# RWKV chain of a hybrid encoder layer: outputs in one group, whole-array products, inverses from 16-row blocks

## The chip, the cores and the metric

The kernel runs on one core of a Trainium2 chip, as one program. The metric is the device time of one execution in microseconds (us), lower is better; three executions of the kernel before are on record, with their median. Engines of the core: TensorE (PE, with its weight loads shown apart as PEld), VectorE (DVE), ScalarE (ACT), GpSimd (POOL) and SyncE (SP, which here only issues DMAs).

## The reference

One layer of an encoder over 256 tokens of width 2048, in float32: a projection, three mixers A, B and C, a gated merge, an output projection and a SwiGLU block. The change touches mixer C alone, RWKV-7 time mixing with 16 heads of 64 channels, once forward and once backward over the tokens:

```python
def step(s, inp):
    r_t, w_t, k_t, v_t, a_t, b_t = inp
    sa = jnp.einsum('dbhij,dbhj->dbhi', s, a_t)
    s = s * w_t[..., None, :] + sa[..., :, None] * b_t[..., None, :] + v_t[..., :, None] * k_t[..., None, :]
    return s, jnp.einsum('dbhij,dbhj->dbhi', s, r_t)
_, y = lax.scan(step, s0, (r, w, k, v, a, b))
...
y = norm_last(y, GN_EPS).reshape(bsz, seq, C_W) * ln_g + ln_b
out = (y + bonus) * g
```

## The kernel before, in words

The kernel has stages in a row: mixer A, mixer B, mixer C (`rwkv`), the last part of the merge (`merge_last`), the output projection, the feed-forward block. Weights come from DRAM in pieces of 128x512 (`wsplit`, L217): SP issues the load, ACT rounds the piece to its high part `wh` (L225), DVE or POOL subtracts to get the low part `wl` (L229). A dense step (`dense`, L233) is three products of 256 columns on the whole array, L242 to L244. Those of mixer C's own projections and of the merge of branch B fill the gaps of the scan: they are called dense below.

The scan is worked out in chunks of 64 tokens, four chunks, for eight pairs of heads (j from 0 to 7), both directions d together. For a pair, in turn:

- `wkv_prep` (L526) makes decays, keys and the arrays `bk` and `ar`; its products L547 use 64 rows of the array, one direction after the other.
- `wkv_scores` (L618) makes the 64x64 score blocks `sc` of all chunks: eight products for a direction (L635), four of one head in 64 rows of the array and then four of the other head; then the blocks go to DRAM (L652).
- `wkv_inverse` (L667) inverts 32x32 diagonal blocks on DVE, a block on a partition: 31 steps k, two instructions each (L688, L689), from a copy `N` loaded at L679. The results go to DRAM (L694), come back as `XX` (L699) and are transposed (L702).
- `wkv_chain` (L707) joins them to 64x64 inverses `XF` by 32x32 products (L731, L742), and then walks the four chunks: L770 (scores times v) and, from the second chunk on, L777 (`ar` times the state) make `Pm`; L785 multiplies by the inverse and gives `UV`; L796 gives what is added to the state, which DVE writes to `sb` (L811, L813); L816 and, from the second chunk on, L819 give the chunk's outputs, which go to `y2` (L824, L826). The products use halves or quarters of the array. L816 and L819 alternate, head by head and direction by direction.
- `wkv_norm` (L833): group norm by two products with a constant (L842, L848), bonus and gate.

These five are generators. `threads` (L481) takes turns between them, and after each yield emits its share of four dense steps a round (`ROUND`), so the order of emission is a round-robin. The framework moves instructions further: the order on an engine is the one that the program ends with. Waits between pieces are the calls of `after`. PSUM tiles come from rings of two, by tag: `big`, `ch`, `inv`, `dn`. `N`, `Y`, `XX`, `UV` have one buffer.

Of the kernel before, what the change touches and what calls it, by code (L numbers as in the profile page):

```python
# [48 lines left out]
for _n, _w in VEC:  # L49
# [6 lines left out]
    ("smask", 256), ("dmask", 64), ("rowm", 2), ("scanm", 257),  # L56
# [11 lines left out]
def shape_constants():  # L68
# [17 lines left out]
    put("rowm", np.stack([blk == 0, blk == 1], 1))  # L86
    put("scanm", np.broadcast_to((np.arange(T + 1) % CH != 0)[None], (P, T + 1)))
# [21 lines left out]
def dft_tables():  # L109
    """odd frequencies (2 k + 1) pi / (2 T), k < T / 2; even and odd samples apart"""  # L110
# [21 lines left out]
def layout(inp):  # L132
# [54 lines left out]
    o["rows"] = np.eye(32).reshape(8, 4, 32).transpose(1, 0, 2)[:, None] * np.ones((1, 32, 1, 1))  # L187
    o["rows"] = o["rows"].reshape(P, 8, 32)
# [5 lines left out]
class Build:  # L194
# [21 lines left out]
    # weights [P, nk, n] from DRAM -> (wh, wl)  # L216
# [16 lines left out]
    def dense(self, ap, xh, xl, ps):  # L233
        """ps[n, t] = sum_k w[k, n] x[k, t]; ap DRAM [P, nk, 128], xh/xl [P, nk, 256]; yields after each k"""
# [48 lines left out]
    def fill(self, n):  # L283
        """emits n steps of the waiting dense products"""
# [26 lines left out]
    def rsqrt_steps(self, x, w, v):  # L311
        """w * -RS_B = x ** -0.5 (x > 0): bit estimate and two Newton steps"""
# [74 lines left out]
    def rwkv(self, rp, ych, ycl, y):  # L387
# [9 lines left out]
        # kd = k (1 + (a - 1) k_a) = k (ka1 (2 a - 1) + ka0)  # L397
# [14 lines left out]
        R["sb"] = []  # L412
        for i in range(2):
            x = rp.tile([P, 2, P], F32, name=f"sb{i}")
            nc.gpsimd.memset(x, 0.0)
            R["sb"].append(x)
# [17 lines left out]
        def more():  # L434
            """the next merge, the queue being short"""
# [45 lines left out]
    def threads(self, live, more):  # L481
        """takes turns between the generators, with dense steps between: more where fewer have something to do"""
# [19 lines left out]
    def weave(self, gens, steps, lead=0):  # L502
        """takes turns between the generators (a pair (n, gen) starts n turns late), with some of `steps` dense ones between"""
# [895 lines left out]
```

## Time and profile before

| | |
|---|---|
| three executions | 2071.43, 2072.45 (median), 2075.77 us |
| span of the profiled execution, first to last instruction | 2081.1 us |
| PE busy in that span | 1985.2 us (95%) |
| DVE busy | 1468.4 us (71%) |
| ACT, POOL busy | 1020.5 us (49%), 552.9 us (27%) |
| mean granted clock of TensorE | 0.965 |

No time of the profiled execution beside its span is on record; the span is 8.65 us above the median of the three. Mixer C's scan lies at about 505 to 1103 us of the span, the merge's last part and everything behind it after 1103 us. A busy PE is not a PE at its peak: a product counts as busy from its start to its end, and its successors overlap it. What a group of products costs is read from starts, not from busy time.

### The profile page before, as it was taken

What the parts mean: (1) busy time and instruction counts of PE and PEld (TensorE: products, weight loads), DVE (VectorE), ACT (ScalarE), POOL (GpSimd) and SP (SyncE); (2) the same over time, 40 slices, a digit from 0 to 9 for tenths busy, and PEclk for the clock granted to TensorE, in tenths of its full rate; (3) what the DMA queues carried; (4) which work ended last, traced back from release to release, by engine and by line L of the source; (5) the groups of instructions that cost most, each with busy time, mean ns of one, the idle gap of its engine ahead of it and who ended that gap; (6) DMA issues with size and microseconds to landing.
All of it is one profiled execution on the core that took longest, in us unless ns stands there. A gap on an engine that the chain in (4) does not pass through costs nothing. (4 is left out here: it accounts for less than half of the span.)

```text
span 2081.1 us, 37899 instructions
## 1 busy us (share of the span) xinstructions
PE 1985.2 (95%) x13636; PEld 1762.9 (85%) x13636; DVE 1468.4 (71%) x2852; ACT 1020.5 (49%) x1982; POOL 552.9 (27%) x557
## 2 busy tenths in 40 slices
PE   7999999999888888999999999999999999999997
PEld 5899999999777777877778888888888888888886
DVE  7968788765887786776766667766666666655555
ACT  5655555545333343333335555555555555544543
POOL 5322322325643443453441121111111111100001
PEclk9999999999888999898899999999999999999998
DMA  7454444345332233332324556555555555566664
GB/s 235 153 173 151 133 161 150 127 157 175 121 103 84 86 106 94 106 103 74 107 91 161 186 197 219 186 191 189 192 189 191 189 190 190 190 186 187 186 187 137
DMA packets 200325, 324.35 MB, mean 156 GB/s; under 512 B 45766, under 2 KB 49352, under 8 KB 200136
## 3 DMA queue, kind: packets, MB, share of 16 engines
q1 hardware_dynamic: 193904, 310.33, 45.9%
q0 software_dynamic: 1888, 5.93, 0.9%
q10 hardware_dynamic: 4344, 5.67, 0.8%
q8 instruction: 107, 1.75, 0.4%
q14 instruction: 82, 0.67, 0.1%
HBM read 317.65 MB, written 4.19 MB: 155 GB/s over the span
## 5 line engine op out<-in xcount | busy, mean ns | idle before, releaser
L225 ACT CAST wh<-w 128x512 fp32r<-128x512 f32 x1148 | 705.0, 619 | 693.8 <-PE ps_dn L262 259.6
L229 DVE TENSOR_TENSOR wl<-w,wh 128x512 fp32r<-128x512 f32 x945 | 709.0, 755 | 370.0 <-ACT wh L225 366.2
L242 PE MATMUL ps_dn<-hw,wh 128*128 128x256 f32 x1328 | 407.4, 307 | 2.3 <-ACT th L1269 1.2
L229 POOL TENSOR_TENSOR wl<-w,wh 128x512 fp32r<-128x512 f32 x203 | 273.2, 1349 | 454.7 <-ACT wh L225 432.2
L244 PE MATMUL ps_dn<-hw,wl 128*128 128x256 f32 x1328 | 388.8, 293 | 1.3 <-DVE wl L229 1.3
L243 PE MATMUL ps_dn<-hw,wh 128*128 128x256 f32 x1328 | 389.7, 293 | 0.0
L242 PEld LDWEIGHTS ps_dn<-hw,wh 128*128 128x128 f32 x1328 | 264.5, 199 | 18.6 <-issue 8.5
L243 PEld LDWEIGHTS ps_dn<-hw,wh 128*128 128x128 f32 x1328 | 265.1, 200 | 4.3 <-issue 1.7
L244 PEld LDWEIGHTS ps_dn<-hw,wl 128*128 128x128 f32 x1328 | 264.7, 199 | 3.7 <-DVE wl L229 1.5
L262 PE MATMUL ps_dn<-gw,wh 128*128 128x512 f32 x704 | 246.3, 391 | 0.0
L262 PE MATMUL ps_big<-gw,wh 128*128 128x512 f32 x704 | 246.0, 391 | 0.0
L262 PE MATMUL ps_dn<-hid,wh 128*128 128x512 f32 x660 | 233.2, 396 | 0.0
L263 PE MATMUL ps_dn<-hid,wl 128*128 128x256 f32 x704 | 198.4, 282 | 0.0
L263 PE MATMUL ps_dn<-gw,wl 128*128 128x256 f32 x704 | 197.3, 280 | 0.0
L263 PE MATMUL ps_big<-gw,wl 128*128 128x256 f32 x704 | 197.1, 280 | 0.0
L262 PEld LDWEIGHTS ps_dn<-gw,wh 128*128 128x128 f32 x704 | 131.7, 187 | 28.9
L262 PEld LDWEIGHTS ps_big<-gw,wh 128*128 128x128 f32 x704 | 131.6, 187 | 28.9
L262 PEld LDWEIGHTS ps_dn<-hid,wh 128*128 128x128 f32 x660 | 124.0, 188 | 30.2
L263 PEld LDWEIGHTS ps_dn<-gw,wl 128*128 128x128 f32 x704 | 133.1, 189 | 0.1
L263 PEld LDWEIGHTS ps_big<-gw,wl 128*128 128x128 f32 x704 | 133.1, 189 | 0.0
L263 PEld LDWEIGHTS ps_dn<-hid,wl 128*128 128x128 f32 x704 | 132.2, 188 | 0.0
L1328 POOL TENSOR_TENSOR acc<-acc,sq 128x256 f32<-128x256 f32 x28 | 20.8, 744 | 291.3 <-ACT sq L1326 283.3
(383 smaller groups left out, 3499.0 us busy)
## 6 DMA issues: line engine op xcount, KB each, us to landing
w<-in_wgu_dram SPq DMA_DIRECT2D x352, 256.0 KB, 3.0
w<-in_wgt_dram SPq DMA_DIRECT2D x192, 256.0 KB, 3.0
w<-in_wdn_dram SPq DMA_DIRECT2D x176, 256.0 KB, 2.9
w<-in_wc_dram SPq DMA_DIRECT2D x108, 256.0 KB, 3.0
w<-in_wb_dram SPq DMA_DIRECT2D x96, 256.0 KB, 3.0
w<-in_wbr_dram SPq DMA_DIRECT2D x96, 256.0 KB, 2.7
w<-in_wo_dram SPq DMA_DIRECT2D x64, 256.0 KB, 3.1
w<-in_wav_dram SPq DMA_DIRECT2D x32, 256.0 KB, 3.9
```

Source lines behind the costliest of these rows:

```text
L225: nc.scalar.copy(wh[:, :m], w[:, :m])
L229: e.tensor_tensor(wl[:, :m], w[:, :m], wh[:, :m].bitcast(F32), ALU.subtract)
L242: mm(ps, wh[:, i, :], xh[:, k, :], start=(k == 0), stop=False)
L243: mm(ps, wh[:, i, :], xl[:, k, :], start=False, stop=False)
L244: mm(ps, wl[:, i, :], xh[:, k, :], start=False, stop=(k == nk - 1))
L262: mm(ps, wh[:, i, :], xk.rearrange("p a t -> p (a t)"), start=(k == 0), stop=False)
L263: mm(ps[:, :T], wl[:, i, :], xk[:, 0, :], start=False, stop=(k == nk - 1))
L1328: self.nc.gpsimd.tensor_tensor(acc, acc, s, ALU.add)
```

## The change

Mixer C alone is changed; line numbers of the changed code differ from those of before.

```diff
-        R["sb"] = []
-        for i in range(2):
-            x = rp.tile([P, 2, P], F32, name=f"sb{i}")
+        R["sb"] = [rp.tile([P, 2, P], F32, name=f"sb{i}") for i in range(3)]
+        R["ar"] = [rp.tile([P, 2, NC_, 3, CH], F32, name=f"ar{i}") for i in range(2)]
+        for x in R["sb"] + R["ar"]:
             nc.gpsimd.memset(x, 0.0)
+        R["d2"] = [self.dp.tile([32, 2, 8, 2, 32], F32, name=f"d2{i}") for i in range(2)]
+        none = rp.tile([P, 256], F32, name="none", tag="kd")
+        nc.gpsimd.memset(none, 0.0)
+        for x in R["d2"]:
+            nc.gpsimd.dma_start(x.rearrange("a b c r e -> (a b c r e)").rearrange("(p f) -> p f", p=P), none)
...
+        pd = [self.pst("big") for _ in range(2)]
+        for i in range(2):
+            for d in range(2):
+                rows = slice(64 * d, 64 * d + 64)
+                nc.tensor.matmul(pd[d][:, i * T:(i + 1) * T], wa[rows, i, :],
+                                 R["lo"][rows, 1 + i, :], start=True, stop=True, tile_position=(64 * d, 0))
...
+            ph = [self.pst("big") for _ in range(2)]
+            for c in range(NC_):
+                for h in range(2):
+                    rows = slice(64 * h, 64 * h + 64)
+                    nc.tensor.matmul(ph[h][:, c * P:(c + 1) * P], bk[rows, d, c // 2, (c % 2) * P:(c % 2) * P + P],
+                                     ar[rows, d, c, 1 - c % 2::1 + c % 2, :], start=True, stop=True, tile_position=(64 * h, 0))
...
-        src = d1.rearrange("d u (q s) e -> (d u q) (s e)", s=32)
+        src = d1.rearrange("d u (q s) e -> (d u q) s e", s=32)
         for i in range(4):
-            D.dma_start(N[32 * i:32 * i + 32].rearrange("p s e -> p (s e)"), src)
+            b = 16 * (i % 2)
+            D.dma_start(N[32 * i:32 * i + 32], src[:, b:b + 16, b:b + 16])
...
-        for k in range(31):
-            n, w = 31 - k, k // 4 + 1
+        for k in range(15):
+            n, w = 15 - k, k // 2 + 1
...
+        V.transpose(Z[:, 1].rearrange("p a b -> p (a b)"), Z[:, 0].rearrange("p a b -> p (a b)"))
+        blocks = [(d, u, q) for d in range(2) for u in range(4) for q in range(4)]
+        ps = self.pst("inv")
+        for d, u, q in blocks:
+            r, o = slice(32 * q, 32 * q + 32), slice(32 * u, 32 * u + 32)
+            nc.tensor.matmul(ps[r, P * d + 32 * u:P * d + 32 * u + 32], Mo[r, d, o], Z[r, 1, d, o], start=True, stop=True,
+                             tile_position=(32 * q, 32 * q))
+        T0 = tl([2, P], "T0")
+        S.copy(T0, ps[:, :2 * P].rearrange("p (d n) -> p d n", d=2))
+        yield 1
...
+            if i:
+                for d, c in at_step(i):
+                    nc.tensor.matmul(pv[:, :P], ar[:, d, c, 0:2, :], R["sb"][i - 1][:, d, :], start=False, stop=(d == 1))
...
+            if i < 3:
+                pv = of_v(i + 1)
...
+                for d, c in at_step(i):
+                    nc.tensor.matmul(ct[:, P * d:P * d + P], bkT[:, d, c, :], UV[:, d, c // 2, c % 2, :], start=True, stop=True)
...
-            for d, c, h in us:
-                o = ct[64 * h:64 * h + 64, 64 * d:64 * d + 64]
-                nc.tensor.matmul(o, UV[:, d, c // 2, c % 2, 64 * h:64 * h + 64], sc[:, d, h, c, CH:], start=True,
-                                 stop=(i == 0), tile_position=(0, 64 * h))
-                if i:
-                    nc.tensor.matmul(o, St[64 * h:64 * h + 64, d, 64 * h:64 * h + 64], ar[64 * h:64 * h + 64, d, c, 1, :],
-                                     start=False, stop=True, tile_position=(64 * h, 64 * h))
...
+        ps = self.pst("big")
+        for i in range(1, NC_):
+            for d, c in at_step(i):
+                nc.tensor.matmul(ps[:, c * CH:(c + 1) * CH], R["sb"][i - 1][:, d, :], ar[:, d, c, 2, :],
+                                 start=(i == 1 and d == 0), stop=False)
+        for i in range(NC_):
+            for d, c in at_step(i):
+                for h in range(2):
+                    nc.tensor.matmul(ps[64 * h:64 * h + 64, c * CH:(c + 1) * CH], UV[:, d, c // 2, c % 2, 64 * h:64 * h + 64],
+                                     sc[:, d, h, c, CH:], start=False, stop=(i == 3 and d == 1), tile_position=(0, 64 * h))
+        y2 = tl([T], "y2")
+        S.copy(y2, ps[:, :T])
```

In words. The outputs of all four chunks are computed behind the chain, in one group: six products with the state on the whole array (L861 in the changed code), then sixteen on halves of the array (L866). The product with the state inside the chain (L819 there) and the one that makes the state's addition (L841 there) use all 128 rows and columns; `ar` has a zero block beside each `a` for that, and the states of three chunks are kept. The products of the two heads (L650 there) and of the two directions (L554 there) alternate between the two halves of the array's rows, into two `big` tiles. `of_v` (L809 there) makes the next chunk's first product right behind the inverse's (L828 there). The inverses are started from 16x16 blocks: 15 steps on DVE instead of 31, loads of `N` in pieces of 16 elements, writes of `d2` in pieces of 16, and two more groups of thirty-two 32x32 products (L730 and L738 there) with a copy on ACT between them, `Mo` being made by two POOL instructions a pair. The gate's product moves from `wkv_prep` to `wkv_norm`, where DVE multiplies by it out of PSUM; POOL did that before. POOL clears `sb`, the two `ar` tiles and `d2` once, ahead of the first pair.

On PE, in the sixth pair, the third chunk of the kernel before reads so (dense rows stand ahead of it and behind):

```order
L244 MATMUL ps_dn<-yb,wl 128x256
L770 MATMUL ps_ch<-UV,sc 64x64 x4
L777 MATMUL ps_ch<-sb_6468,ar 64x128
L816 MATMUL ps_ch<-sc,UV 64x64
L819 MATMUL ps_ch<-ar,sb_6470 64x64
L816 MATMUL ps_ch<-sc,UV 64x64
L819 MATMUL ps_ch<-ar,sb_6470 64x64
L816 MATMUL ps_ch<-sc,UV 64x64
L819 MATMUL ps_ch<-ar,sb_6470 64x64
L816 MATMUL ps_ch<-sc,UV 64x64
L819 MATMUL ps_ch<-ar,sb_6470 64x64
L777 MATMUL ps_ch<-sb_6468,ar 64x128
```

The outputs stood between the products of the two directions with the new state, L777. In the changed program the same place of PE holds only the inverse's product and the next chunk's first one, and then four dense steps:

```order
L245 MATMUL ps_dn<-hw,wl 128x256
L828 MATMUL ps_inv<-T_11902,xf 64x64 x4
L809 MATMUL ps_ch<-UV,sc 64x64 x4
L243 MATMUL ps_dn<-hw,wh 128x256
L244 MATMUL ps_dn<-hw,wh 128x256
L245 MATMUL ps_dn<-hw,wl 128x256
```

L841 and L819 follow in the same way, two rows of 128x128 each, with four dense steps behind each. What moved is the output group, which now stands behind the pair's last chunk on PE:

```order
L245 MATMUL ps_dn<-hw,wl 128x256
L861 MATMUL ps_big<-ar_6472,sb_6468 128x64 x2
L861 MATMUL ps_big<-ar_6472,sb_6469 128x64 x2
L861 MATMUL ps_big<-ar_6472,sb_6470 128x64 x2
L866 MATMUL ps_big<-sc,UV 64x64 x16
L243 MATMUL ps_dn<-hw,wh 128x256
```

At the end of the scan 27 dense steps stand behind the last gate product (L891 in the changed code). On SP, the loads of the first pair's blocks read so before:

```order
L652 DMA d_7114<-Md 128x4x32
L652 DMA d_7114<-Mu 128x4x32
L224 DMA w<-in_wc_dram 128x512 x2
L679 DMA N<-d_7114 32x1024 x4
L224 DMA w<-in_wc_dram 128x512 x5
```

And in the changed program, at the same place of SP:

```order
L670 DMA d_7125<-Md 128x4x32
L670 DMA d_7125<-Mu 128x4x32
L225 DMA w<-in_wc_dram 128x512
L701 DMA N<-d_7125 32x16x16 x4
L225 DMA w<-in_wc_dram 128x512 x5
```

The four loads of `N` stay four, behind the same stores; each moves 32x16 pieces of 16 elements where it moved 32 pieces of 1024.

## Rows read from the trace of the kernel before

**Rows 1.** The page: TensorE's granted clock in 40 slices, tenths.
```profile
PEclk9999999999888999898899999999999999999998
```
**Rows 2.** Windows: length, busy us (instructions) of PE, PEld, DVE, ACT, POOL; clock, DMA.
```profile
505.00:1103.00 598.00, 537.20 (x4453) 459.86 (x4452) 446.06 (x1145) 217.15 (x476) 264.89 (x255) 0.90 0.32 98
```
**Rows 3.** Lines of PE, 505 to 1103 us: busy, mean ns, idle before, releasers.
```profile
L816 PE MATMUL ps_ch<-sc,UV 128*64 128x64 f32 x256 | 37.7, 259 | 9.1 <-DVE sb L811 6.1 <-DVE sb L813 2.0 <-ACT UV L791 0.7
...
L777 PE MATMUL ps_ch<-sb,ar 128*64 128x128 f32 x96 | 19.8, 332 | 9.0 <-DVE sb L811 7.4 <-DVE sb L813 1.7
```
**Rows 4.** Timeline of PE: start us, us, engine, line; a state's addition among dense products.
```profile
1021.70 0.28 PE L242 MATMUL ps_dn<-yb,wh 128*128 128x256 f32 x1
1021.82 0.28 PE L243 MATMUL ps_dn<-yb,wh 128*128 128x256 f32 x1
1022.03 0.46 PE L796 MATMUL ps_ch<-UV,bkT 128*64 128x64 f32 x8
1022.42 0.39 PE L244 MATMUL ps_dn<-yb,wl 128*128 128x256 f32 x1
1022.64 0.28 PE L242 MATMUL ps_dn<-yb,wh 128*128 128x256 f32 x1
```
**Rows 5.** Timeline of PE: the outputs of one chunk.
```profile
1050.94 0.33 PE L816 MATMUL ps_ch<-sc,UV 128*64 128x64 f32 x2
1051.19 0.33 PE L819 MATMUL ps_ch<-ar,sb 64*64 64x64 f32 x2
...
1053.21 0.28 PE L244 MATMUL ps_dn<-yb,wl 128*128 128x256 f32 x1
```
**Rows 6.** Timeline of PE: both kinds of 64x64 products together.
```profile
1086.12 0.27 PE L770 MATMUL ps_ch<-UV,sc 64*64 64x64 f32 x2
1086.14 0.27 PE L785 MATMUL ps_ch<-Pm,xf 64*64 64x64 f32 x2
...
1086.74 0.28 PE L243 MATMUL ps_dn<-hw,wh 128*128 128x256 f32 x1
```
**Rows 7.** Timeline of PE: four transposes of 128 columns on the whole array.
```profile
579.19 0.60 PE L661 MATMUL ps_big<-consts,bk 128*128 128x128 f32 x4
...
579.74 0.28 PE L243 MATMUL ps_dn<-hw,wh 128*128 128x256 f32 x1
```
**Rows 8.** Timeline of PE: the scores of one direction.
```profile
856.63 1.88 PE L635 MATMUL ps_big<-ar,bk 64*128 64x128 f32 x16 [2.08 <-DVE sc L637]
...
858.67 0.28 PE L243 MATMUL ps_dn<-hw,wh 128*128 128x256 f32 x1
```
**Rows 9.** Timeline of PE: the products of one direction's decays.
```profile
886.40 1.13 PE L547 MATMUL ps_big<-lo,wa 64*128 64x256 f32 x4
...
887.68 0.28 PE L243 MATMUL ps_dn<-hw,wh 128*128 128x256 f32 x1
```
**Rows 10.** Timeline of PE: sixteen 32x32 products, two passes each.
```profile
1072.56 0.45 PE L742 MATMUL ps_inv<-XX,T 32*32 32x32 f32 x32
...
1073.17 0.28 PE L244 MATMUL ps_dn<-hw,wl 128*128 128x256 f32 x1
```
**Rows 11.** Lines of DVE, 505 to 1103 us: busy, mean ns, idle before.
```profile
L689 DVE TENSOR_TENSOR Y<-Y,Yt 128x60 f32<-128x60 f32 (+24 forms) x248 | 95.1, 383 | 4.0
```
**Rows 12.** Timeline of DVE: the state of one chunk.
```profile
1088.02 1.19 DVE L811 SCALAR_TENSOR_TENSOR sb<-ps_ch,E,ws 64x64 f32<-64x64 f32 x4 [0.96 <-PE ps_ch L796]
```
**Rows 13.** Tile N: durations ns min/median/max, first and last start us; landing of its loads.
```profile
L688 DVE TENSOR_TENSOR Yt<-N,Y x248: 142/214/4892, 563.7 to 1059.1; 128x60 f32<-128x60 f32 x12, 128x54 f32<-128x54 f32 x8, 128x66 f32<-128x66 f32 x8, 128x28 f32<-128x28 f32 x8
L679 SPq DMA_DIRECT2D N<-d x32: 325/420/597, 554.9 to 1013.8; - x32
...
DMA to landing us min/median/max: 2.1/3.4/6.2
```
**Rows 14.** DMA issues, 505 to 1103 us: KB each, median us to landing.
```profile
XX<-d SPq DMA_DIRECT2D x8, 128.0 KB, 3.3
...
d<-Md SPq DMA_DIRECT2D x8, 64.0 KB, 1.8
```

More of the change, by code (lines that the diff above doesn't have):

```diff
@@ L186, in layout @@
     o["cst"], o["csw"] = shape_constants()
-    o["rows"] = np.eye(32).reshape(8, 4, 32).transpose(1, 0, 2)[:, None] * np.ones((1, 32, 1, 1))
-    o["rows"] = o["rows"].reshape(P, 8, 32)
+    o["rows"] = np.eye(16).reshape(8, 2, 16).transpose(1, 0, 2)[:, None] * np.ones((1, 64, 1, 1))
+    o["rows"] = o["rows"].reshape(P, 8, 16)
     o["feat"] = filter_features()
@@ L542, in wkv_prep @@
         sm = self.cst("scanm")
-        for d in range(2):
-            rows = slice(64 * d, 64 * d + 64)
-            ps = self.pst("big")
-            for i in range(2):
-                nc.tensor.matmul(ps[:, i * T:(i + 1) * T], wa[rows, i, :],
-                                 R["lo"][rows, 1 + i, :], start=True, stop=True, tile_position=(64 * d, 0))
+        pd = [self.pst("big") for _ in range(2)]
[4 more added lines that the diff above has]
+                                 R["lo"][rows, 1 + i, :], start=True, stop=True, tile_position=(64 * d, 0))
+        for d in range(2):
+            ps = pd[d]
             tw = tl([T], "tw")
@@ L760, in wkv_chain @@
         self.passed.add(("v", j))
[L763 to L782 removed]
+        at_step = lambda i: [(d, i if d == 0 else 3 - i) for d in range(2)]
@@ new lines, in wkv_chain @@
+        pv = of_v(0)
+        for i in range(NC_):
+            if i:
+                for d, c in at_step(i):
+                    nc.tensor.matmul(pv[:, :P], ar[:, d, c, 0:2, :], R["sb"][i - 1][:, d, :], start=False, stop=(d == 1))
+            Pm = tl([P], "T1")
+            V.tensor_copy(Pm, pv[:, :P])
+            yield 1
+            ct = self.pst("inv")
+            for h in range(2):
+                for d, c in at_step(i):
+                    hb = 1 - c % 2
+                    rows = slice(64 * hb, 64 * hb + 64)
+                    nc.tensor.matmul(ct[rows, 64 * h:64 * h + 64], XF[rows, d, h, c // 2, :, :],
+                                     Pm[rows, 64 * h:64 * h + 64], start=True, stop=True, tile_position=(64 * hb, 64 * hb))
+            if i < 3:
+                pv = of_v(i + 1)
+            for d, c in at_step(i):
@@ L783, in wkv_chain @@
                 hb = 1 - c % 2
                 rows = slice(64 * hb, 64 * hb + 64)
-                nc.tensor.matmul(ct[rows, P + 64 * h:P + 64 * h + 64], XF[rows, d, h, c // 2, :, :],
-                                 Pm[rows, 64 * h:64 * h + 64], start=True, stop=True, tile_position=(64 * hb, 64 * hb))
-            for d in range(2):
-                c = i if d == 0 else 3 - i
-                hb = 1 - c % 2
-                rows = slice(64 * hb, 64 * hb + 64)
-                (S.copy if d else V.tensor_copy)(UV[rows, d, c // 2, c % 2, :], ct[rows, P:2 * P])
+                (S.copy if d else V.tensor_copy)(UV[rows, d, c // 2, c % 2, :], ct[rows, :P])
@@ L792, in wkv_chain @@
             yield 1
             if i < 3:
[L794 to L802 removed]
+                ct = self.pst("inv")
@@ L848, in wkv_norm @@
         nc.tensor.matmul(ps[:, :T], self.cst("bones"), sq2, start=True, stop=True)
+        pg = self.pst("big")
+        nc.tensor.matmul(pg[:, :T], g2, R["lo"][:, 0, :], start=True, stop=True)
         yield 1
```

138 lines of the change are left out of this document (65 added, 73 removed).

## The prediction

> **What bounds the kernel now.** First the granted clock over the span: it dips below full in the second quarter and is full behind it [rows 1]. That stretch is mixer C's scan, so the windows are asked for it alone: of 598 us PE is busy 537.2, so it stands idle for 60.8 us; DVE is busy 446.06, ACT 217.15, POOL 264.89, at a mean clock of 0.90 [rows 2]. PE is the busiest, but it is not full of dense work. The dense products there are 720 steps of three (24 columns of weights of mixer C and 16 of the merge, less what is emitted ahead of the first pair), and one product follows another after 0.12 us at full clock [rows 4]; that makes 259 us. The other half of the stretch goes to the scan's small products, to waits, and to the lower clock. The clock has two levels, 1.2 and 2.4 GHz; a mean of 0.90 says that a fifth of the stretch ran at the lower. So the question is what a small group costs the dense stream, and for that the timeline of PE is read by starts, at full clock, among dense products.
>
> I count as the price of a group the time from its start to the start of the second dense product behind it, less 0.12 for that product's own place, plus 0.09 for the entry where the array is divided. The entry is seen in [rows 4]: the group starts 0.21 us behind a dense product instead of 0.12. Its price is 0.61 - 0.12 + 0.09 = 0.58 for eight passes (a float32 product is two). The outputs of one chunk, sixteen passes, cost 2.27 - 0.12 + 0.09 = 2.24 [rows 5]: the two kinds of products alternate, and a new kind starts 0.25 us behind the last. Sixteen passes of two kinds on different quarters, which start 0.02 us apart, cost 0.62 - 0.12 + 0.09 = 0.59, as much as eight [rows 6]. Four passes of 128 columns on the whole array cost 0.55 - 0.12 = 0.43, 0.11 each, taken without an entry [rows 7].
>
> **The change part by part.** *The chain.* Before, a pair has four groups L785, three L796, four L770, two times three L777 and the first chunk's L816: 18 groups, at 0.58 10.4 us; with three output groups of 2.24 it is 17.1. Where two groups stand together one entry is paid, so I take 16.3. After: the first L809 and the last L828 0.58 each; three groups of L828 with L809, between 0.59 (both kinds at once, [rows 6]) and 1.16 (one behind the other), I take 0.8; L841 and L819 three times each, four passes on the whole array, 0.43 [rows 7]. Outputs: twelve passes of 64 columns on the whole array, each between half of the 0.11 and 0.11, together 0.6 to 1.3, I take 1.0; 32 passes on halves, between 1.2 (sixteen couples at 0.06 and one entry and exit of 0.25) and four groups of 0.58, 2.3; they stand together as eight passes do in [rows 4], so I take 1.3. Sum 0.58 + 0.58 + 2.4 + 2.6 + 2.3 = 8.5. Saved 7.8 a pair, 62 us in all (bounds 6.2 and 9 a pair).
>
> The Trainium skill, "TensorE: Matmul & The Clock Gate", section "LDWEIGHTS (loading the stationary operand)", speaks against whole-array products here: a load's time goes by the columns of weights, so a block with another head's half in it pays for all 128. By its rate a pass of the state's output would cost 0.107 us whatever the 64 columns that stream, 1.3 us for twelve, and the sum would be 2 us lower. [Rows 7] agree with that rate at 128 columns; no row here shows 64 columns behind 128 of weights.
>
> *Scores.* One direction costs 2.04 - 0.12 + 0.09 = 2.01 [rows 8], 0.11 a pass with 0.25 for entry and exit. Alternating between halves of the rows the sixteen passes are eight couples: 8 x 0.11 + 0.25 = 1.13 if the halves run at once as the quarters do in [rows 6], 2.01 if not. I take 1.13: 0.88 twice a pair, 14 us in all; bound 0. *Decays.* A direction costs 1.28 - 0.12 + 0.09 = 1.25 [rows 9]; both in one group of four couples cost about one of them: 10 us saved, and 2 if only an entry goes.
>
> *Inverses.* On PE two groups of 64 passes are new. Thirty-two passes cost 0.61 - 0.12 + 0.09 = 0.58 [rows 10]; 64 between that and 1.16, I take 0.95: 15 us more in all. On DVE 32 instructions a pair go, 256 of some 0.38 us (L689 [rows 11]; L688, its twin, has half of the instructions): 97 of its 446 us. The new transpose, addition and gate product are some 0.4 us each, and four small additions to the outputs go: nothing in sum.
>
> PE's work at full clock falls by 62 + 14 + 10 - 15 = 71 us. Divided by the stretch's 0.90 it is 79 (bounds: 33 / 0.9 = 37 with every upper price, 87 / 0.9 = 97 with every lower).
>
> *Waits.* PE's idle 60.8 us: the outputs waited 9.1 us, mostly for the state on DVE [rows 3]; they now stand behind the chain, where the states are long there. Of the other 51.7 most are waits for DVE, whose work shrinks by a fifth: 11 us less. Against it stands an added wait. L819 of the changed code needs the states of both directions; before, the outputs' 2.24 us stood between the two halves of L777, which still waited 9.0 us [rows 3]. DVE's four instructions take 1.19 us [rows 12], and four dense steps, 1.44 us, now stand between L841 and L819. That covers them when DVE is free; where another thread's work stands ahead of them, all that is queued on PE, dense products too, waits up to another 1.19 us. In 24 chunks that is 0 to 29 us; I take 10, as the threads other than the chain have work for about a third of the rounds. Waits: -9 - 11 + 10 = -10, bounds -30 and +20.
>
> *At nothing.* The gate's product only moves on PE. POOL's clearing at the start: a mean POOL instruction takes 264.89 / 255 = 1.04 us, so even at three times that for each of the two large ones, with the stores behind them, it is under 10 us once; POOL is idle for half of the stretch and weights are split three pieces ahead; without that cover PE would wait those 10 us. The last pair's norm is covered by the dense steps behind it, 27 x 0.36 = 9.7 us.
>
> **Sum.** 79 + 10 = 89 us. Against the profiled span: 2081.1 - 89 = 1992. That span is 8.65 us above the median; the same 89 off the median give 2072.45 - 89 = 1983, rounded up to 1984. The likeliest case's own range is 1955 to 2015: prices from 60 to 97, waits from -20 to +5.
>
> **Rivals.** *The waits take it back* (1 in 6). With less small work between them, the chain's links (copy of `Pm`, `UV`, state) wait for DVE and ACT more often. For: every link is a round, and a round has four dense steps whatever else is in it; [rows 8] show a wait of 2.08 us for a `big` tile, and the scores now take both `big` tiles at once. Against: DVE loses 97 us. At 50 us of new waits the time is 2034.
>
> *The clock opens* (1 in 8). At the lower level the stretch loses about a tenth of its time. For: the clock is full in the quarter behind it [rows 1], where PE does nothing but whole-array work, and much of the divided-array work goes. Against: waits of 2 us stay. If half of the lower-clock time goes, another 25 us and some of the waits' bound go with it: 1950.
>
> *Slower: the loads of N* (1 in 12). A load of `N` moves the same blocks in 2048 pieces of 64 bytes, where it was 128 long ones. DVE is in order, so if `N` lands late, the chain's copies behind the first L709 wait, and PE for them. Today a load lands after 3.4 us (at most 6.2) and DVE starts on it 563.7 - 554.9 = 8.8 us behind its issue [rows 13]. Stores and loads in small pieces: 512 pieces land in 1.8 us, 1024 in 3.3 [rows 14], so 1.5 us for 512 more, and 2048 would take 6.3: inside the 8.8. To eat 89 us over eight pairs each load must be 11 us late, that is land after 20. At 22 us the time is 2072.45 - 89 + 8 x (22 - 8.8) = 2089. The Trainium skill, "DMA: Bandwidth & Descriptors", section "Specifications", is the reason to list it: it wants pieces of 512 bytes or more and says that smaller ones are read, modified and written. By that alone the loads are several times dearer; the trace's store of 128-byte pieces that lands in 1.8 us bears the rule out only weakly.
>
> *Nothing* (1 in 33): a cause outside PE's order holds the stretch; ACT at 217 of 598 us and the loads do not look like one [rows 2]. Time 2072.
>
> **How the numbers follow.** Forecast 0.6, waits 0.17, clock 0.12, nothing 0.03, slower 0.08. A measurement of this kernel tells 0.2%, 4 us, from no change. The waits' case is faster but for a small part: faster 0.88, same 0.04, slower 0.08. The range reaches from 1945 (half of the clock's case) to 2035 (half of the waits' case); outside are about 0.05 below and 0.15 above.
>
> **What would show it.** Right: the scan's stretch falls from 598 us to about 509; the output group costs 2 to 3 us once a pair; L650 starts in couples; L819's wait stays under 20 us in all; DVE's busy time there falls by nearly 100. Wrong: the stretch's idle time on PE above 80 us, L650 with starts 0.11 apart one by one, the first L709 idle for a DMA, or the clock's mean far from 0.90 either way.

## The result and the profile after

Four executions of the changed kernel took 2008.69 to 2020.24 us, median 2014.29; the kernel before, beside it, 2073.57. The ratio is 0.9715, 95% interval 0.9683 to 0.9747: faster by 59 us, where 89 were forecast, and inside the range. A second set of six executions (after_again, below) gave 0.9692 (0.9667 to 0.9716), 64 us. The spans of the profiled executions, 2018.2 us and 2081.1 before, differ by 62.9. A profile is of one execution, and those of the changed kernel lie up to 14 us apart (both of its profiles are of the slowest), so a few microseconds between two profiles tell little.

The granted clock by slices, from the page of the changed kernel, answers to [rows 1]:

```profile
PEclk8999999999889899898999999999999999999999
```

The scan now ends at 1039.2 us, where the first product of the merge's last part starts; it ended at 1103. Its window, with the columns of [rows 2]:

```profile
505.00:1039.20 534.20, 472.05 (x5275) 430.62 (x5274) 374.65 (x885) 213.32 (x453) 269.66 (x281) 0.91 0.35 101
```

The reader is to see three things. The whole gain lies here: 598.0 - 534.2 = 63.8 us, and what follows takes 979.0 us against 978.1. PE's busy time fell from 537.20 to 472.05, by 65.2. Its idle time did not fall: 60.8 before, 534.2 - 472.05 = 62.2 after. DVE lost 71.4 us of busy time, and the mean clock is 0.91 against 0.90.

Busy time is not work when the clock changes. By the clock rows of the traces PE was busy at the lower of its two levels, 1.2 GHz, for 121.1 us before and 82.6 after. With that time counted half, PE's work at full clock is 537.2 - 60.5 = 476.7 us before and 472.1 - 41.3 = 430.8 after. So the 63.8 us are 46 of PE's work, 19 of less time at the lower level, and -1.4 of idle time.

PE's lines in that window, with the idle time ahead of each and what ended it, answer to [rows 3]:

```profile
L650 PE MATMUL ps_big<-ar,bk 64*128 64x128 f32 x256 | 36.0, 327 | 7.4 <-DVE bon L625 5.7 <-DVE bk L610 1.2 <-ACT ta L561 0.3
L819 PE MATMUL ps_ch<-sb,ar 128*128 128x128 f32 x96 | 21.3, 330 | 17.8 <-DVE sb L853 14.9 <-DVE sb L855 2.6
L841 PE MATMUL ps_inv<-UV,bkT 128*128 128x128 f32 x96 | 17.7, 306 | 11.6 <-DVE UV L835 11.6
...
L730 PE MATMUL ps_inv<-Z,Mo 32*32 32x32 f32 x512 | 6.6, 204 | 8.0 <-DVE Z L725 8.0
```

The state's addition to `Pm` (L819) waits 17.8 us, as much as the outputs and L777 waited together, 9.1 + 9.0. The waits for `UV` (L841) and for the returned inverses `Z` (L730) make 19.6 of the other 44.4 us; the rest is spread over many lines, none above 7.4 us.

The output group of a pair, from PE's timeline, answers to [rows 5]:

```profile
1022.49 1.45 PE L861 MATMUL ps_big<-ar,sb 128*128 128x64 f32 x12
1023.87 1.15 PE L866 MATMUL ps_big<-sc,UV 128*64 128x64 f32 x32
1024.95 0.39 PE L243 MATMUL ps_dn<-hw,wh 128*128 128x256 f32 x1
1025.17 0.28 PE L244 MATMUL ps_dn<-hw,wh 128*128 128x256 f32 x1
```

By the prediction's measure (to the second dense product, less its 0.12) it costs 1025.17 - 1022.49 - 0.12 = 2.56 us, once a pair. Twelve whole-array passes take 1.38, or 0.115 each with the change of kind: 64 streamed columns did not make these passes cheaper than the 0.11 of 128 columns in [rows 7]. By the Trainium skill's page "TensorE: Matmul & The Clock Gate", section "LDWEIGHTS (loading the stationary operand)", a weight load's time goes by the columns of weights, for 128 of them an estimate of 0.107 us. The trace agrees with that.

The scores come in two ways. From the same timeline, half of a group of one direction whose heads do not alternate, and then a whole group whose heads do, answer to [rows 8]:

```profile
943.93 1.16 PE L650 MATMUL ps_big<-ar,bk 64*128 64x128 f32 x8
945.02 0.38 PE L243 MATMUL ps_dn<-yb,wh 128*128 128x256 f32 x1
...
954.66 1.17 PE L650 MATMUL ps_big<-ar,bk 64*128 64x128 f32 x16
955.76 0.39 PE L243 MATMUL ps_dn<-hw,wh 128*128 128x256 f32 x1
955.98 0.28 PE L244 MATMUL ps_dn<-hw,wh 128*128 128x256 f32 x1
```

Sixteen passes take 1.10 us as couples, eight take 1.09 one by one. Seven of the 16 groups alternate from end to end, two in part, seven not at all: the program alternates, but the order that the framework ends with lets the first head's products pass and holds the second's. I read that as places where only one `big` tile is free; it is not shown by itself. The order on PE in such a place (tile numbers kept; in the trace one begins at 645.32 us):

```
4219 L650 MATMUL ps_big_8399<-ar0_6471,bk_8246 128x128
4220 L828 MATMUL ps_inv_8370<-T1_8352,xf_8192 64x64 x4
4221 L650 MATMUL ps_big_8399<-ar0_6471,bk_8246 128x128 x3
...
4231 L650 MATMUL ps_big_8400<-ar0_6471,bk_8246 128x128 x4
```

The inverse's two lines on DVE, answering to [rows 11], and then tile `N`, answering to [rows 13]:

```profile
L710 DVE TENSOR_TENSOR Y<-Y,Yt 128x30 f32<-128x30 f32 (+10 forms) x120 | 47.3, 394 | 2.7
L709 DVE TENSOR_TENSOR Yt<-N,Y 128x30 f32<-128x30 f32 (+10 forms) x120 | 34.4, 286 | 10.8 <-DMA N<-d 8.6
```

```profile
L709 DVE TENSOR_TENSOR Yt<-N,Y x120: 145/184/1260, 561.7 to 980.6; 128x30 f32<-128x30 f32 x24, 128x14 f32<-128x14 f32 x16, 128x24 f32<-128x24 f32 x16, 128x15 f32<-128x15 f32 x8
...
DMA to landing us min/median/max: 2.1/2.8/3.6
```

The two lines take 81.7 us for the 187.8 of before (95.1, and 92.7 of L688); an instruction is hardly shorter in the mean, though most take 0.18. The loads in 64-byte pieces land after 2.8 us, the long ones after 3.4; each also moves a quarter of the bytes, 32 KB where it was 128.

### The profile page after: what moved, and what is told of

Read it like the earlier page. It is cut to its first block, busy times and chain, and to the rows that moved or that the text cites. A ratio compares the mean times of both kernels' runs of the same rounds, so it can differ in the third digit from the quotient of the medians.

```text
span 2018.2 us, 39307 instructions
## 1 busy us (share of the span) xinstructions
PE 1920.9 (95%) x14468; PEld 1734.5 (86%) x14468; DVE 1397.8 (69%) x2588; ACT 1017.0 (50%) x1958; POOL 562.2 (28%) x587
## 4 chain that ended last, share of the span: by engine, by line
PE 82%; DVE 11%; DMA 3%; issue 2%; ACT 1%; SPq 0%; POOL 0%; DVEq 0%; ACTq 0%; POOLq 0%
PE ps_dn L263 23%; PE ps_dn L264 12%; PE ps_dn L243 9%; PE ps_big L263 8%; PE ps_dn L244 8%; PE ps_dn L245 8%; PE ps_big L264 4%; DVE Y L710 2%; PE ps_big L650 1%; DVE wl L230 1%; DVE Yt L709 1%; DMA Z<-d 1%; PE ps_ch L819 1%; PE ps_big L981 0%; DMA N<-d 0%
## 5 line engine op out<-in xcount | busy, mean ns | idle before, releaser
L230 DVE TENSOR_TENSOR wl<-w,wh 128x512 fp32r<-128x512 f32 x945 | 711.4, 758 | 381.6 <-ACT wh L226 377.8
L243 PE MATMUL ps_dn<-hw,wh 128*128 128x256 f32 x1328 | 402.5, 303 | 1.6 <-ACT th L1312 1.2
L245 PE MATMUL ps_dn<-hw,wl 128*128 128x256 f32 x1328 | 382.9, 288 | 1.9 <-DVE wl L230 1.9
L244 PE MATMUL ps_dn<-hw,wh 128*128 128x256 f32 x1328 | 381.9, 288 | 0.0
L230 POOL TENSOR_TENSOR wl<-w,wh 128x512 fp32r<-128x512 f32 x203 | 273.3, 1350 | 383.9 <-ACT wh L226 345.0
L243 PEld LDWEIGHTS ps_dn<-hw,wh 128*128 128x128 f32 x1328 | 259.5, 195 | 12.4 <-issue 4.0
L245 PEld LDWEIGHTS ps_dn<-hw,wl 128*128 128x128 f32 x1328 | 259.5, 195 | 3.2 <-DVE wl L230 2.1
L244 PEld LDWEIGHTS ps_dn<-hw,wh 128*128 128x128 f32 x1328 | 259.7, 196 | 1.4
```

What stands on the lines that cost most here:

```text
L230: e.tensor_tensor(wl[:, :m], w[:, :m], wh[:, :m].bitcast(F32), ALU.subtract)
L243: mm(ps, wh[:, i, :], xh[:, k, :], start=(k == 0), stop=False)
L244: mm(ps, wh[:, i, :], xl[:, k, :], start=False, stop=False)
L245: mm(ps, wl[:, i, :], xh[:, k, :], start=False, stop=(k == nk - 1))
```

## The experiments

The table puts them together. The scan's length is taken from the first start of the decays' product to the end of the scan in each profile, since the stage ahead ends up to 4 us earlier or later; busy and idle are PE's in the window from 505 us to that end, and "at 1.2 GHz" is the part of the busy time that the clock rows put at the lower level. What follows the scan takes 975 to 979 us, but 986.2 in inverse_fine and 984.8 in score_couples, so their windows end early. Two profiles of one kernel, changed and after_again, differ by 4 us of busy and 5 of idle time.

| kernel | ratio to before (95%) | median us | scan us | PE busy | at 1.2 GHz | PE idle | DVE busy | clock |
|---|---|---|---|---|---|---|---|---|
| before | 1 | 2072.5 to 2078.1 | 591.5 | 537.2 | 121.1 | 60.8 | 446.1 | 0.90 |
| changed | 0.9715 (0.9683 to 0.9747) | 2014.3 | 528.8 | 472.1 | 82.6 | 62.2 | 374.7 | 0.91 |
| after_again | 0.9692 (0.9667 to 0.9716) | 2010.5 | 529.5 | 467.9 | 69.4 | 67.0 | 378.0 | 0.93 |
| heads_apart | 0.9763 (0.9742 to 0.9783) | 2027.5 | 533.2 | 468.9 | 69.0 | 66.8 | 376.6 | 0.93 |
| score_couples | 0.9935 (0.9912 to 0.9959) | 2065.1 | 568.7 | 470.5 | 87.7 | 102.1 | 381.2 | 0.90 |
| score_claim | 0.9711 (0.9689 to 0.9734) | 2011.9 | 523.6 | 454.6 | 69.8 | 70.5 | 371.1 | 0.92 |
| outputs_by_chunk | 0.9766 (0.9746 to 0.9785) | 2027.2 | 538.9 | 496.8 | 58.4 | 46.4 | 375.8 | 0.94 |
| outputs_whole_by_chunk | 0.9706 (0.9677 to 0.9735) | 2019.2 | 530.2 | 471.0 | 56.5 | 65.3 | 382.8 | 0.94 |
| inverse_32 | 0.9835 (0.9813 to 0.9857) | 2040.9 | 551.9 | 473.1 | 96.4 | 83.1 | 444.7 | 0.90 |
| inverse_few | 0.9566 (0.9542 to 0.9589) | 1983.7 | 493.6 | 445.4 | 32.5 | 51.2 | 339.8 | 0.96 |
| few_outputs_by_chunk | 0.9706 (0.9683 to 0.9728) | 2012.8 | 527.0 | 496.5 | 69.4 | 36.4 | 336.7 | 0.93 |
| inverse_fine | 0.9746 (0.9720 to 0.9773) | 2023.1 | 522.3 | 457.4 | 70.8 | 66.0 | 374.5 | 0.92 |
| links_on_act | 0.9731 (0.9709 to 0.9753) | 2017.5 | 529.3 | 459.2 | 69.4 | 71.7 | 362.1 | 0.92 |
| splits_on_pool | 0.9782 (0.9755 to 0.9810) | 2029.9 | 541.9 | 471.7 | 79.7 | 75.8 | 366.0 | 0.91 |

**First theory.** The gain is PE's own work: the output group and the whole-array products. The inverses are worth nothing or less, since PE pays for what DVE saves, and the scores' couples are lost. The rival: the lighter DVE makes the gain. Each part was undone by itself.

*outputs_by_chunk.* The grouped outputs go back into the chain, with a copy or an addition for each chunk and direction behind them (not shown; the cuts of code here and below are shortened):

```diff
+            po = self.pst("ch")
+            for h in range(2):
+                for d, c in at_step(i):
+                    nc.tensor.matmul(o, UV[...], sc[:, d, h, c, CH:], ..., tile_position=(0, 64 * h))
+                    if i:
+                        nc.tensor.matmul(o, R["sb"][i - 1][64 * h:64 * h + 64, d, ...], ar[...], ..., tile_position=(64 * h, 64 * h))
-        for i in range(1, NC_):        # the group at the end
```

> The changed kernel with the outputs computed chunk by chunk again, the two kinds of products alternating, the state's on a quarter, as before the change. My theory: three chunks' groups of 2.24 us and one of 0.58 take the place of one group of 2.57, 4.7 us a pair, 38 us at full clock, 42 at 0.91, and their waits for the state come back, up to 9 us: 2050 to 2065. Rival, that the gain comes from the lighter VectorE: under 15 us, 2014 to 2029.

It costs 0.9766 - 0.9715 or - 0.9692, 11 to 15 us, far from 42. Its window, with the columns of [rows 2], and the state's addition there (L820, the changed kernel's L819), from the lines of PE:

```profile
505.00:1048.20 543.20, 496.81 (x5363) 441.82 (x5361) 375.75 (x915) 214.77 (x476) 267.60 (x281) 0.94 0.36 99
```

```profile
L820 PE MATMUL ps_ch<-sb,ar 128*128 128x128 f32 x96 | 17.0, 296 | 2.7 <-DVE sb L856 1.9 <-DVE sb L854 0.3
```

It waits 2.7 us and not 17.8. PE is busy for 25 us more and idle for 16 us less: the dear outputs stood between the state's product and its use, and hid DVE's work on it. At full clock PE's work is 496.8 - 29.2 = 467.6 us, 37 more than the changed kernel's 430.8 and 34 more than after_again's 433.2: what the first theory had, 38. What paid it back is the idle time, 16 to 21 us, and less time at the lower level, worth 6 to 12. The rival's number was met (2027.2 in 2014 to 2029), but not by its cause: DVE is as busy as before (375.8 for 374.7).

*inverse_32.* The 32-row inverses of before, and nothing else:

```diff
-        for k in range(15):
-            n, w = 15 - k, k // 2 + 1
+        for k in range(31):
+            n, w = 31 - k, k // 4 + 1
...
-        ps = self.pst("inv")           # T0 = Mo Z, XX = Z + T0 Z
```

> The changed kernel with the 32-row inverses of before the change: 31 steps of two VectorE instructions a pair, no new products on PE. My theory: PE loses two groups of 64 passes, 0.87 us each, 14 us at full clock, 15 at 0.91; VectorE gains 70 us of busy time, which gives waits of 5 to 20 us back: 2005 to 2020, that is, this part of the change is worth nothing or less. Rival, that the gain comes from the lighter VectorE: 2040 to 2070.

The first theory falls: 25 to 30 us slower (0.9835 against 0.9715 and 0.9692), the lower edge of the rival's number. DVE has 70 us more and PE 21 us more of idle time. The window, and then the state's addition (L791 here), which has 14 of the 21 us, in the lines of PE:

```profile
505.00:1061.20 556.20, 473.08 (x4243) 430.38 (x4242) 444.68 (x1121) 210.10 (x442) 263.97 (x264) 0.90 0.35 105
```

```profile
L791 PE MATMUL ps_ch<-sb,ar 128*128 128x128 f32 x96 | 23.8, 342 | 31.9 <-DVE sb L825 23.2 <-DVE sb L827 8.5
```

PE's busy time is no lower without the new products (473.1 against 472.1), though they take 12.5 us from start to start in the changed kernel (L730 and L738): the mean clock is 0.90, and the heads of the scores stand apart in nine groups, not seven.

*heads_apart.* The loop over heads outside again:

```diff
-            for c in range(NC_):
-                for h in range(2):
+            for h in range(2):
+                ps = self.pst("big")
+                for c in range(NC_):
```

> The changed kernel with the scores' two heads one after the other again, as before the change. My theory: the couples were lost already, since in 9 of the 16 groups the order on PE does not alternate the heads, and the scores' price fell by nothing (34.2 us of starts after, 33.5 before); so 2014 plus or minus 6 us. Rival, the prediction's own term: the couples saved 0.88 us twice a pair, 14 us at full clock, so 2028 to 2032.

Slower by 10 to 15 us by the ratios, by 4 in the profiles, which are of one execution each. So the groups that do alternate are worth something, between 4 and 15; the reading that the term was lost whole was wrong. It is not a plain return to before, though: by starts at full clock the scores' products take 32.6 us here, 27.5 in the changed kernel and 29.4 in the kernel before.

*score_couples* and *score_claim* force the alternation. The first makes a group of products one unit for the framework, the second claims one tile by a copy of one column and fixes the order of the passes:

```diff
+            with self.tc.tile_critical():
             for c in range(NC_):
```

```diff
+            S.copy(ph[0][:, 0:1], self.cst("ones", 0, 1))
-                for h in range(2):
+                for h in (1, 0):
+                    with (self.tc.issue_after(last.ins) if last is not None else ExitStack()):
```

> The changed kernel with the eight products of a direction's scores held together, so that both heads' tiles must be free before the first and the heads alternate in all 16 groups. My theory: a group of couples costs 1.28 us for sixteen passes where heads apart cost 2.0, so 9 groups times 0.75 us, 6 to 8 us at full clock: 2004 to 2009, with L650's mean start to start falling from 134 ns to about 85. Rival: the wait for the second tile takes it back; the idle time ahead of L650, 7.4 us in the changed kernel, grows to 15 or more and the time stays at 2010 to 2018.

> The changed kernel with the heads of the scores alternating in 15 of 16 groups without holding other work: ScalarE writes one column into one head's tile, and the eight products follow in a fixed order, the other head's first, so the group starts when both tiles are free. Theory: L650's full-clock price falls to 1.28 in all groups, 6 us less at full clock, idle ahead of the scores at most 3 us more: 2004 to 2010 against 2010 to 2014. Rival: the wait for the second tile, or the extra ScalarE copy, gives the 6 us back: 2011 to 2020.

The unit made things worse, and not by the wait for a tile. Lines of PE in score_couples:

```profile
L651 PE MATMUL ps_big<-ar,bk 64*128 64x128 f32 x256 | 25.1, 353 | 28.9 <-DMA w<-in_wbr_dram 10.9 <-DMA w<-in_wc_dram 5.3 <-DMA w<-in_wgt_dram 4.7
```

It waits for the loads of weights that its products don't use, so this run tells nothing of couples. In score_claim 15 of 16 groups alternate, and the scores take 23.2 us from start to start where they took 33.0 in after_again. The idle time rose from 67.0 to 70.5, ahead of the scores from 7.3 to 12.2, and the time did not move: 0.9711, inside the intervals of the changed kernel, though in the one profile the scan is 6 us shorter. The rival's number holds (2011.9 in 2011 to 2020).

**Second theory.** The links of the chain wait for what stands ahead of them in DVE's queue; so DVE's work is part of the bound and PE's savings are partly given back. The timeline of DVE in the changed kernel ahead of one copy of `UV`, the inverse's blocks in front:

```profile
855.74 0.19 DVE L709 TENSOR_TENSOR Yt<-N,Y 128x30 f32<-128x30 f32 x1
855.85 0.69 DVE L230 TENSOR_TENSOR wl<-w,wh 128x512 fp32r<-128x512 f32 x1
856.46 0.18 DVE L710 TENSOR_TENSOR Y<-Y,Yt 128x30 f32<-128x30 f32 x1
...
858.83 0.29 DVE L562 TENSOR_SCALAR tw<-tw 128x256 f32<-128x256 f32 x1
859.15 0.69 DVE L564 TENSOR_TENSOR_SCAN cum<-wconsts,tw 128x256 f32<-128x256 f32 x1
859.87 0.29 DVE L835 COPY UV<-ps_inv 64x128 f32<-64x128 f32 x1
```

And PE at that moment:

```profile
860.22 0.58 PE L841 MATMUL ps_inv<-UV,bkT 128*128 128x128 f32 x1 [3.71 <-DVE UV L835]
```

*inverse_few* leaves out 12 of the 15 inverse steps; *few_outputs_by_chunk* does the same to outputs_by_chunk:

```diff
-        for k in range(15):
+        for k in range(3):
```

> The changed kernel with 3 of the 15 steps of the 16-row inverses, so 24 of a pair's 30 VectorE instructions are left out and the output is not the reference's. It takes some 60 us of VectorE's 375. Theory, the links wait for what stands queued ahead of them on VectorE: 70 us of VectorE work were worth 21 us of PE's idle time and 25 us of time in inverse_32, so here idle falls from 62 to 40 to 48 us and the time to 1990 to 2000. Rival, that what is left are latencies of the links and of the DMA: idle 55 to 62 and 2008 to 2016.

> The outputs by chunk of outputs_by_chunk, and 3 of the 15 inverse steps of inverse_few (so work is left out and the output is not the reference's). Undone with all the steps, the output group was worth 10 to 17 us, though PE's busy time changed by 25 to 29. Theory, two queues share the bound: PE's saving was paid back in waits for VectorE; with 24 VectorE instructions a pair out of the way the same edit costs 20 to 30 us against inverse_few's 1983.7, so 2004 to 2014. Rival, that the output group's work hides the state's link by its length alone, whatever VectorE does: the same 10 to 17 us, 1994 to 2001.

inverse_few is 27 us faster than after_again beside it, where the theory said 10 to 20; idle fell by 16 us to 51.2, where it said 40 to 48, and DVE's busy time by 38, not 60. The clock, 0.96 for 0.93, gave what waits did not. The wait for the state did not fall. Two of PE's lines in after_again, and then in inverse_few:

```profile
L819 PE MATMUL ps_ch<-sb,ar 128*128 128x128 f32 x96 | 20.5, 320 | 16.7 <-DVE sb L853 13.8 <-DVE sb L855 2.6
L841 PE MATMUL ps_inv<-UV,bkT 128*128 128x128 f32 x96 | 18.5, 315 | 12.0 <-DVE UV L835 11.9
```

```profile
L819 PE MATMUL ps_ch<-sb,ar 128*128 128x128 f32 x96 | 19.6, 310 | 17.7 <-DVE sb L853 16.1 <-DVE sb L855 0.7
L841 PE MATMUL ps_inv<-UV,bkT 128*128 128x128 f32 x96 | 16.1, 287 | 7.2 <-DVE UV L835 6.9 <-ACT UV L835 0.2
```

What fell are the waits for `UV`, here, and for `Z` (L730), from 10.9 to 3.3. The window of inverse_few, and then that of few_outputs_by_chunk:

```profile
505.00:1001.60 496.60, 445.43 (x5255) 409.03 (x5255) 339.80 (x691) 212.84 (x451) 269.85 (x281) 0.96 0.39 108
```

```profile
505.00:1037.80 532.80, 496.42 (x5375) 444.34 (x5374) 336.68 (x725) 216.23 (x478) 269.86 (x282) 0.93 0.38 102
```

With DVE out of the way the outputs by chunk cost 0.9706 - 0.9566, 29 us: the theory's number, but not by its mechanism. The idle time that the outputs hide is 15 us, as in the full kernel (16), and PE's work at full clock is 33 us more (461.8 for 429.2), as there (34 to 37). What differs is the time at the lower level: it rises from 32.5 to 69.4 us, worth 18, where in the full kernel it fell. So the hiding goes by the outputs' presence, as the rival said, and the larger price comes with the clock.

*after_again*, *outputs_whole_by_chunk*, *inverse_fine.* The second puts cheap outputs behind L841, the third lets the inverse give way after every second step:

```diff
+            if i:
+                for d, c in at_step(i):
+                    nc.tensor.matmul(po[:, 64 * d:64 * d + 64], R["sb"][i - 1][:, d, :], ar[:, d, c, 2, :], ...)
+            for d, c in at_step(i):
+                for h in range(2):
+                    nc.tensor.matmul(po[64 * h:64 * h + 64, ...], UV[...], sc[:, d, h, c, CH:], ..., tile_position=(0, 64 * h))
```

```diff
-            if k % 4 == 3:
+            if k % 2 == 1:
```

> The changed kernel once more, unaltered, as the ground that the others of this set are held against: 0.968 to 0.975 of the kernel before.

> The changed kernel with the outputs by chunk, behind L841, but cheap: the state's first, on the whole array, then the eight passes on halves; so the state's link has work to hide it and the two kinds don't alternate. Theory, cover: three groups of 0.44 + 0.6 = 1.05 us and one of 0.6 stand for one of 2.57, 1.2 us a pair more, 10 us in all, and about half of the 15.6 us of idle time that the dear outputs by chunk took away stays away, as they are half as long: 2010 to 2018. Rival, that any work between the links hides them wholly: idle 46 us and 2003 to 2010. Rival, that only PE's own work counts: idle stays at 62 us and the time is 10 us up, 2022 to 2028.

> The changed kernel with the inverse giving way after every second step, not every fourth, so blocks of four VectorE instructions (some 1.4 us) and not of eight (2.7) can stand ahead of a link. Theory, queued blocks: the longest waits of 2.5 to 3.7 us fall to about 2 and idle by 10 us, 2002 to 2010. Rival, that the same instructions merely stand elsewhere, or that the inverse ends four rounds later and delays the chain: 2012 to 2030.

In outputs_whole_by_chunk the wait at the state's addition falls from 17.8 to 9.6 us, but the wait for `Pm` on DVE rises from 3.6 to 11.4; idle stays at 65.3 and the interval covers the changed kernel's. The wait moved one link on. PE's work at full clock is 442.7 us, 10 to 12 more than in the changed kernel, as forecast; less time at the lower level paid it back. So none of the three cases came true whole. In inverse_fine the longer scan used up the dense steps: its window ends with the last pair's chain unfinished and 986.2 us behind it, not 979. Idle is the same and the kernel slower: the rival's second form.

*links_on_act* and *splits_on_pool* take work off DVE:

```diff
-            V.tensor_copy(Pm, pv[:, :P])
+            S.copy(Pm, pv[:, :P])
-                (S.copy if d else V.tensor_copy)(UV[...], ct[rows, :P])
+                S.copy(UV[...], ct[rows, :P])
```

```diff
-        self.pool_share = 0.6
+        self.pool_share = 1.0
```

> The changed kernel with the copies of Pm (L821) and of UV (L835, both directions) on ScalarE: 64 copies of 0.29 us leave VectorE, 64 of 0.26 join ScalarE, which is busy 213 of 535 us. Theory, queued blocks on VectorE make the links late: the idle time ahead of L841 (11.9 us) and L828 (4.0) falls to under 5 in all, that ahead of L819 by some us, together 10 to 15 us less idle and 1996 to 2004. Rival: the copies now stand behind ScalarE's weight casts, 0.62 us each, and each other; idle stays within 5 us of 67 and the time at 2008 to 2016.

> The changed kernel with every weight's low part (L230) taken on POOL in this stage, where two of nine now stand on VectorE: 40 instructions of 0.78 us leave VectorE, 31 us, and with them 13 waits for ScalarE's casts in which VectorE's queue stood still for 19.9 us; POOL gets 40 times 1.3 us and is then busy 320 of 530 us. Theory, the chain's links wait for what stands ahead of them on VectorE: in inverse_few 38 us of VectorE's busy time were worth 16 us of idle time on PE and 27 us in all; so here idle falls from 67 to 40 to 52 us, the time to 1985 to 1998. Rival: POOL's splits now come late, and the dense products wait for them: idle time ahead of L245, 1.9 us now, of 15 us or more, and 2008 to 2025.

Both miss. In links_on_act the waits for `Pm` and `UV` are gone, and the other two take them over. PE's waits there (us in total, times, longest):

```profile
PE ps_ch L819 <- DVE sb L853: 24.2, 9, 5.0
PE ps_inv L730 <- DVE Z L725: 15.4, 6, 3.9
```

In splits_on_pool dense products wait for no weights, so its rival falls too; yet PE's idle time rose from 67.0 to 75.8 us. DVE lost 40 instructions of 0.78 us, 31 us, but only 12 us of busy time. Its timeline shows why, one instruction of the inverse, and beside it POOL's:

```profile
562.17 5.33 DVE L709 TENSOR_TENSOR Yt<-N,Y 128x26 f32<-128x26 f32 x1
567.54 0.18 DVE L710 TENSOR_TENSOR Y<-Y,Yt 128x26 f32<-128x26 f32 x1
```

```profile
561.83 0.73 POOL L1319 TENSOR_TENSOR macc<-macc,th 128x256 f32<-128x256 f32 x1
562.51 4.94 POOL L230 TENSOR_TENSOR wl<-w,wh 128x512 fp32r<-128x512 f32 x4
```

The DVE instruction of 0.18 us took 5.33: it ended when POOL's row of five was over, at 562.51 + 4.94 = 567.45. No version here that does all the work beats the changed kernel by more than the intervals; less work for POOL in this stage was not tried.

## Why the prediction was right, and where its sizes were off

**The sum.** PE's work at the stretch's clock was to fall by 79 us and fell by 65.2 of busy time. The waits were to fall by 10 and rose by 1.4. At full clock PE's work was to fall by 71 us and fell by 46; the clock gave 19, where the division by 0.90 allows 8. By starts at full clock, idle time left out, PE's products make this table. A group's entry and exit, which the prediction books in the group, stand here with the dense products.

| products | forecast | before | after | saved |
|---|---|---|---|---|
| outputs | 40 | 49.8 | 20.3 | 29.5 |
| rest of the chain | 22 | 50.2 | 41.1 | 9.1 |
| scores | 14 | 29.4 | 27.5 | 1.9 |
| decays | 10 | 17.7 | 10.1 | 7.6 |
| new products of the inverses | -15 | 0 | 10.1 | -10.1 |
| dense, with entries and exits | | 303.6 | 296.0 | 7.6 |
| others | 0 | 25.9 | 25.3 | 0.6 |
| sum | 71 | 476.6 | 430.4 | 46.2 |

Point by point:

- *Prices of single groups: right.* L861 with L866 cost 2.56 us for the forecast 1.0 + 1.3, since 64 streamed columns cost as much as 128, which I had weighed and taken half of. By the same measure L841 costs 0.44 and L819 0.45 for 0.43, L828 with L809 0.60 for 0.8 (medians at full clock).
- *The chain as a whole, 62 us: mis-sized.* Outputs and rest save 39 us, and at most 46 with all that the dense products lost. Which part of the working was off is not shown.
- *Output group: work right within about a quarter, its worth mis-sized.* The working makes 40 us at full clock, 45 in the stretch, and 9 for the wait that goes, against 10 for L819's new wait. Undone, PE's work rises by 34 to 37 us, but the time by only 11 to 15. I priced the outputs as work alone; they were also the cover of the state's link. I did see that "the outputs' 2.24 us stood between the two halves of L777", but called four dense steps cover enough and put 10 us against it. The idle time that the outputs hid is 16 us or more, and with them PE spent less time at the lower level.
- *Inverses: mis-sized, the other way.* They were to cost 15 us on PE (12.5 from start to start, 10.1 at full clock: about right) and give back 11 of waits. Undone, they are worth 25 to 30. The 11 us took a fifth of the waits for a fifth less of DVE's work; measured, 70 us of DVE's work carried 21 us of idle time. The inverse's own lines lost 106 us, for 97 forecast. Some 43 of these were waits for POOL (last section): 68 instructions of over 0.8 us took 86.3 us before, 24 took 32.9 after, where the medians are 0.21 and 0.18. DVE as a whole lost 71 of busy time. By the sum of its instructions' durations it lost 90, as new and longer instructions took back 16; the other 19 are durations that overlapped in the record before. The 0.38 us is a mean that holds waits: the median in [rows 13] is 0.21.
- *Scores, 14 us: mis-sized.* The couples run at once, at 955.98 - 954.66 - 0.12 + 0.09 = 1.29 for the 1.13 forecast, but in 7 of 16 groups and parts of two; elsewhere the starts stand 0.11 apart one by one, a sign of being wrong by the prediction itself. PE's price fell by 1.9 us. Undone, it is worth 4 to 15 us, in a program whose scores cost more than those of before; made whole in score_claim, where they take 17.4, it brought nothing.
- *Decays and the rest:* L547's 18.7 us from start to start became L554's 11.7, 7 less where 10 were forecast. The three parts undone singly make 11 + 25 + 10 = 46 of 59 us, or 15 + 30 + 15 = 60 of 64, if they may be added. So 4 to 13 us are left for the decays and the rest of the chain, 17 of PE's work in the table, where the working has 62 - 40 + 10 = 32 at full clock. These were not undone by themselves.
- *The rivals.* Little was late through `N`: 2.8 us to land where the working had 6.3, and DVE's first L709 waited 8.6 us in all, twice. The working has a load move "the same blocks"; it moves a quarter of the bytes. The page "DMA: Bandwidth & Descriptors" of the Trainium skill, section "Specifications", puts pieces under 512 bytes below line rate; with a quarter of the bytes these loads landed sooner than the long ones (3.4), so no run here tests it. The clock opened in part: PE's time at the lower level fell from 121.1 to 82.6 us, with the mean at 0.91, and further in inverse_few (32.5, 0.96). "The waits take it back" came true in part: idle time stood 11 us above the forecast, at the links named, for DVE and not for ACT.

The likeliest case's own range ends, by its terms, at 2072.45 - 60 + 5 = 2017 and not at 2015; the measured 2014.3 lies in either.

So the total came out within the range, 25 to 30 us from the forecast, in part by luck. PE's work fell by 25 us less and the waits by 11 less than forecast, and the clock made up 11. Of the parts, the outputs gave less than forecast, and the inverses, which the sum has as a loss of some 5 us, gave 25 to 30. That the outputs acted through PE's wait for the state is shown (17.8 us to 2.7). That DVE's load acts through PE's waits is shown too, at the state in inverse_32 and at `UV` and `Z` in inverse_few. Why the time at the lower level falls in one run and rises in the other stays open.

## What to carry to other kernels

Before moving dear work out of a chain of links, ask what wait it hides, and price the move as work minus cover. Where two in-order engines hand a chain back and forth, undo each part of a change by itself: relief on the engine that is not the busiest can be worth more than PE's own savings. Where the clock changes within a stretch, compare work at full clock, idle time and time at the lower level one by one: busy time alone hid here that the outputs' work came back almost whole. A mean duration far above its median was here a wait inside the instruction; price with the median, and look for what the rest waits for.

## What the runs showed of the hardware

A short DVE instruction with two SBUF inputs that begins within one of POOL's mostly ends with POOL's work: in the changed kernel 46 of L709 and L710 began while POOL's instruction had over 0.25 us to go, and 44 did not end before it. There 24 of them took over 0.8 us where the median is 0.18; each ended 0.02 to 0.07 us behind the end of a weight split on POOL (L230), by their starts and durations in the trace. In splits_on_pool there are 37, 50.9 us together, and all end so. The timeline of DVE in the changed kernel, and then POOL's:

```profile
807.08 3.22 DVE L710 TENSOR_TENSOR Y<-Y,Yt 128x35 f32<-128x35 f32 x1
```

```profile
806.99 0.69 POOL L612 TENSOR_TENSOR ar<-kk,E 128x256 f32<-128x256 f32 x1
807.63 0.73 POOL L1319 TENSOR_TENSOR macc<-macc,th 128x256 f32<-128x256 f32 x1
808.32 0.68 POOL L612 TENSOR_TENSOR ar<-kk,E 128x256 f32<-128x256 f32 x1
808.96 1.28 POOL L230 TENSOR_TENSOR wl<-w,wh 128x512 fp32r<-128x512 f32 x1
```

DVE waited through four POOL instructions in a row and ended at 810.30, POOL at 810.24. The Trainium skill's page "SBUF — State Buffer", section "Who interferes with whom", says that a DVE instruction with two SBUF inputs and a GpSimd instruction that reads SBUF exclude each other, the second blocking until the first is done; the rows agree, and in them the turn did not come between POOL's instructions.
